# One store of a convolution cut into transfers of 112, 8 and 8 channels

## The chip, the cores and the metric

The kernel runs on one core of one Trainium2 chip. The metric is the device time of one execution in microseconds (us), and the time of a kernel is the median of several executions. TensorE (PE) multiplies, VectorE (DVE) adds, ScalarE (ACT) copies, GpSimd (POOL) casts and adds, and SyncE (SP) waits and issues transfers. The core has 16 DMA engines; SP, ACT and POOL each issue transfers into a queue of their own, and the same 16 engines serve all queues.

## The reference

A 3x3 convolution with padding 1, batch of 16 images, 64 input channels, 128 output channels, 64x64 pixels, in float32:

```python
x_pad = np.pad(x, ((0, 0), (0, 0), (1, 1), (1, 1)), mode='constant')
for b, co, ci, kh, kw:
    output[b, co] += weight[co, ci, kh, kw] * x_pad[b, ci, kh:kh+h, kw:kw+w]
```

(the five loops are written on one line here). The input is 16.8 MB, the output 33.6 MB.

## The kernel before

**The work and its tiling.** Images are worked on in eight pairs (`p` from 0 to 7). The two images of a pair lie in the two halves of the 128 partitions, 64 input channels each. Two output rows are made at a time from shared products: the middle row of the weights meets the sum of two neighbouring input rows (tile `ss`, made by POOL, or by DVE for the first pair), and the other products use differences of the weights' rows, made once at the start (`Wt`). A pair's 32 double rows are done in four blocks of eight.

**One block** (lines 129 to 190). Three groups of matmuls: `U` from the row sums, `A` for the upper rows, `Bt` for the lower rows. ACT copies `U` of both images from PSUM to SBUF (line 173). DVE adds it to `A` (line 183) and to `Bt` (line 186) and writes the output tile `ots[b2]`, 128 output channels by 64 rows by 64 columns in float32, 16 KB for each channel. There is one such tile for each image.

**Input.** SP issues the loads of the weights and of the first two pairs in float32 (lines 41 to 46). POOL issues the other six pairs, cast to 16 bits on the way (line 56), all of them in the first 8 us of the span.

**Output.** Each image is 2 MB. `cuts_of` (lines 112 to 114) says after which block which rows are stored: pairs 0 to 5 store each image whole after the last block; pair 6 stores its first image in two halves and its second whole; pair 7 stores both in halves. The first image of a pair is stored by SP right away (line 188). The second image's store is put on the list `held` (line 190) and issued by ACT in the next block, after ACT's pair of copies (lines 175 and 176), or after the last block (lines 191 and 192):

```python
while held:
    keep(store(nc.scalar, *held.pop(0)))
```

`keep` holds an instruction at its written place among those of its engine. So the second image of the sixth pair (`p` = 5) is issued by ACT in the first block of pair 6. Output tiles come from a pool of seven buffers; the tile of the sixth pair's second image is not used again by a later one. Each transfer raises a semaphore by 16 as its engines land; eight such semaphores go round among the transfers that SP and ACT issue, and at the end of the program (line 218) SP waits for all stores to have landed.

Of the kernel before, what the change touches and what calls it, by code (L numbers as in the profile page):

```python
# [13 lines left out]
def kernel(  # L14
# [8 lines left out]
    CO = weight.shape[0]  # L23
    assert H == 64 and W == 64 and CI == 64 and CO == 128 and B % 2 == 0
    NP = B // 2
# [4 lines left out]
    out_rows = out.rearrange("b co h w -> b co h w")  # L30
# [34 lines left out]
    def sums(eng, p, src, lo, n):  # L65
        if p not in ss:
            ss[p] = spool.tile([128, H // 2, W], F16, tag="ss", name="ss")
        v = src.rearrange("p (j i) c -> p j i c", i=2)
        keep(
            eng.tensor_add(  # L70
                ss[p][:, lo : lo + n, :], v[:, lo : lo + n, 0, :], v[:, lo : lo + n, 1, :]
            )
        )
# [21 lines left out]
    def cast(copy, p, src, lo, hi):  # L95
        keep(copy(xs[p][:, lo:hi, :], src[:, lo:hi, :]))  # L96
# [13 lines left out]
    held = []  # L110
# [2 lines left out]
    halves = {1: (0, 32), 3: (32, 64)}  # L113
    cuts_of = [(whole, whole)] * (NP - 2) + [(halves, whole), (halves, halves)]

    def store(eng, p, b2, ot, lo, hi):
        return eng.dma_start(
            out_rows[2 * p + b2, :, lo:hi, :],
            ot.rearrange("p j i c -> p (j i) c")[:, lo:hi, :],
        )  # L120

    for p in range(NP):
        if p + 1 < NP:
            for lo in (0, 16):
                sums(nc.gpsimd, p + 1, x1 if p == 0 else xs[p + 1], lo, 16)
        ots = [
            opool.tile([128, H // 2, 2, W], F32, tag="ot", name="ot") for _ in range(2)
        ]
        for blk in range(4):
            j0 = blk * RB  # L130

            def group(wi_rows):

                tiles = [
                    psum.tile([128, RB, W], F32, tag="acc", name="acc") for _ in range(2)
                ]
                n = 3 * len(wi_rows)
                i = 0
                for wi, off in wi_rows:
                    for kw in (1, 0, 2):  # L140
                        c_lo, c_hi = max(0, 1 - kw), min(W, W + 1 - kw)
                        for b2 in range(2):
                            p0 = 64 * b2
                            lo, hi = j0, j0 + RB
                            if off is None:
                                rhs = ss[p][p0 : p0 + 64, lo:hi, c_lo + kw - 1 : c_hi + kw - 1]
                            else:
                                while 2 * lo + off < 0:
                                    lo += 1
                                while 2 * (hi - 1) + off > H - 1:  # L150
                                    hi -= 1
                                first = 2 * lo + off
                                last = 2 * (hi - 1) + off
                                rhs = xs[p][
                                    p0 : p0 + 64,
                                    first : last + 1 : 2,
                                    c_lo + kw - 1 : c_hi + kw - 1,
                                ]
                            nc.tensor.matmul(  # L159
                                tiles[b2][:, lo - j0 : hi - j0, c_lo:c_hi],  # L160
                                Wt[p0 : p0 + 64, wi, kw, :],
                                rhs,
                                start=i == 0,
                                stop=i == n - 1,
                            )
                        i += 1
                return tiles

            U = group([(G1, None)])
            us = []  # L170
            for b2 in range(2):
                ut = upool.tile([128, RB, W], F32, tag="ut", name="ut")
                keep(nc.scalar.copy(ut, U[b2]))  # L173
                us.append(ut)
            while held:
                keep(store(nc.scalar, *held.pop(0)))
            for piece in later.get((p, blk), ()):
                cast(nc.scalar.copy, *piece)
            if p == 0 and blk < 3:
                sums(nc.vector, 0, x0, j0 + RB, RB)  # L180
            A = group([(G21, 1), (G0, -1)])
            for b2 in range(2):
                nc.vector.tensor_add(ots[b2][:, j0 : j0 + RB, 0, :], A[b2], us[b2])  # L183
            Bt = group([(G01, 0), (G2, 2)])
            for b2 in range(2):
                nc.vector.tensor_add(ots[b2][:, j0 : j0 + RB, 1, :], Bt[b2], us[b2])  # L186
            if blk in cuts_of[p][0]:
                store(nc.sync, p, 0, ots[0], *cuts_of[p][0][blk])
            if blk in cuts_of[p][1]:
                held.append((p, 1, ots[1], *cuts_of[p][1][blk]))  # L190
    while held:
        keep(store(nc.scalar, *held.pop(0)))

# [29 lines left out]
```

## Time and profile before

| | |
|---|---|
| median of 3 runs | 126.64 us (126.49 to 126.67) |
| the profiled execution | 126.7 us |
| its span, first to last instruction | 124.9 us |
| PE busy | 107.1 us (86%) |
| DVE busy | 83.4 us (67%) |
| ACT busy | 43.0 us (34%) |
| POOL busy | 36.9 us (30%) |
| queue q1 (issued by SP) | 2016 packets, 21.27 MB, 41.2% of 16 engines |
| queue q10 (issued by ACT) | 1296 packets, 16.78 MB, 31.7% |
| queue q0 (issued by POOL) | 864 packets, 6.29 MB, 24.3% |
| a whole image, ACT's queue: issue to landing | 18.2 us |
| a half image, ACT's queue: issue to landing | 8.3 us |

Engines' busy time leaves out what their sequencers do, such as issuing transfers. A queue's share is the time that its packets took, over the span of 16 engines. A packet of a store is one channel's contiguous row, 16 KB of a whole image or 8 KB of a half; the transfer ends with a packet of 4 bytes on each engine, which raises the semaphore. Two more queues, q8 and q14, bring instructions: seven packets of 16 KB and some of 8 KB over the span.

### The profile page before, as it was taken

The page shows a single profiled execution, that of the slowest core. Times are in us where ns is not written, and L with a number is a line of the kernel's source. Part 1 is how long each engine was busy: PE and PEld are TensorE (multiplying, and loading weights), DVE is VectorE, ACT ScalarE, POOL GpSimd, SP SyncE. Part 2 cuts the span into 40 slices and gives each one's busy share as a digit, 9 for nine tenths or more (in the row PEclk, how much of TensorE's full clock was granted, in tenths as well). Part 3 has the DMA queues.
Part 4 walks back from the last instruction along what each step waited for, and adds up shares of the span by engine and source line. Part 5 has one row for each costly group of instructions (what it writes and reads, how often), then busy time and mean ns, then how long its engine had stood idle before and what let it go on. Part 6 is the DMA issues. An engine that isn't in the chain of part 4 may idle for free.

```text
span 124.9 us, 2408 instructions
## 1 busy us (share of the span) xinstructions
PE 107.1 (86%) x978; PEld 53.9 (43%) x978; DVE 83.4 (67%) x134; ACT 43.0 (34%) x74; POOL 36.9 (30%) x29
## 2 busy tenths in 40 slices
PE   0489997399999999999999999999999999998000
PEld 0334443144545545555455555555555555553000
DVE  0135998227778777878877887877787778768200
ACT  4284234466333333333333333333333333333000
POOL 2845101999929101910048000750000000000000
PEclk9999999779999999999999999999999999999955
DMA  4999999999999999999999999999999999999991
GB/s 119 353 362 320 325 336 218 212 278 341 378 370 320 325 380 349 346 372 336 357 367 357 328 378 420 441 420 430 435 420 430 420 420 420 443 425 417 401 407 66
DMA packets 4187, 44.48 MB, mean 356 GB/s; under 512 B 465, under 2 KB 465, under 8 KB 721
## 3 DMA queue, kind: packets, MB, share of 16 engines
q1 hardware_dynamic: 2016, 21.27, 41.2%
q10 hardware_dynamic: 1296, 16.78, 31.7%
q0 software_dynamic: 864, 6.29, 24.3%
q8 instruction: 7, 0.11, 0.3%
q14 instruction: 4, 0.02, 0.0%
HBM read 17.07 MB, written 33.55 MB: 405 GB/s over the span
## 4 chain that ended last, share of the span: by engine, by line
PE 72%; DMA 15%; POOL 2%; DVE 1%; SPq 1%; issue 1%; DVEq 0%
PE acc L159 72%; DMA x<-in_x_dram 15%; POOL ss L70 2%; SPq L44 1%; DVE ot L183 1%; DVEq L218 0%; DVE ot L186 0%; SPq L41 0%; DVEq L183 0%
## 5 line engine op out<-in xcount | busy, mean ns | idle before, releaser
L159 PE MATMUL acc<-xs,Wt 64*128 64x504 f16 (+3 forms) x768 | 89.0, 379 | 0.0
L159 PEld LDWEIGHTS <-Wt 64*128 64x128 f16 x960 | 52.8, 96 | 56.2 <-issue 6.8
L183 DVE TENSOR_TENSOR ot<-acc,ut 128x512 f32<-128x512 f32 x64 | 41.2, 685 | 24.0 <-PE acc L159 21.7
L173 ACT COPY ut<-acc 128x512 f32<-128x512 f32 x64 | 34.4, 590 | 63.3 <-issue 41.7
L186 DVE TENSOR_TENSOR ot<-acc,ut 128x512 f32<-128x512 f32 x64 | 41.1, 683 | 0.0
L70 POOL TENSOR_TENSOR ss<-xs 128x1024 f16<-128x1024 f16 x12 | 25.2, 2125 | 31.7 <-DMA xs<-in_x_dram 31.7
L159 PE MATMUL acc<-ss,Wt 64*128 64x504 f16 (+1 forms) x192 | 27.6, 392 | 3.5 <-POOL ss L70 2.7
L70 DVE TENSOR_TENSOR ss<-x 128x512 f16<-128x512 f32 x4 | 2.7, 685 | 9.0 <-DMA x<-in_x_dram 9.0
L96 ACT CAST xs<-x 128x1024 f16<-128x1024 f32 (+1 forms) x6 | 6.3, 1067 | 3.1 <-DMA x<-in_x_dram 3.1
L70 POOL TENSOR_TENSOR ss<-x 128x1024 f16<-128x1024 f32 x2 | 4.7, 2344 | 8.4 <-DMA x<-in_x_dram 8.4
L88 PE MATMUL wp<-ident,w 128*64 128x128 f16 x18 | 1.3, 328 | 4.4 <-POOL w L50 4.4
L56 POOL DMA_DIRECT2D xs<-in_x_dram x6 | 3.3, 582 | 0.0
L96 POOL CAST xs<-x 128x1024 f16<-128x1024 f32 (+1 forms) x2 | 2.4, 1248 | 3.0 <-DMA x<-in_x_dram 3.0
L88 PEld LDWEIGHTS <-w 128*64 128x64 f16 x18 | 1.1, 210 | 4.4 <-POOL w L50 4.4
L90 ACT CAST Wt<-wp 128x384 f16<-128x384 f32 x1 | 0.5, 478 | 3.1 <-PE wp L88 3.1
L90 ACT ACT_TABLE_LOAD x1 | 1.3, 1283 | 0.7 <-PEq L207 0.7
L50 POOL CAST w<-w_raw 128x576 f16<-128x576 f32 x1 | 0.7, 663 | 2.4 <-DMA w_raw<-in_weight_dram 2.4
L99 ACT CAST Wt<-wp 128x384 f16<-128x384 f32 x1 | 0.5, 478 | 0.5 <-DVE Wt L93 0.5
L92 DVE TENSOR_TENSOR Wt<-wp,Wt 128x384 f16<-128x384 f32 x1 | 0.6, 550 | 0.0
L93 DVE TENSOR_TENSOR Wt<-wp,Wt 128x384 f16<-128x384 f32 x1 | 0.5, 547 | 0.0
L100 ACT CAST Wt<-wp 128x384 f16<-128x384 f32 x1 | 0.5, 485 | 0.0
masks.py:199 POOL TENSOR_SCALAR_AFFINE_SELECT ident<-ident 128x128 f16<-128x128 f16 x1 | 0.3, 292 | 0.1
(5 smaller groups left out, 0.6 us busy)
## 6 DMA issues: line engine op xcount, KB each, us to landing
out_dram<-ot ACTq DMA_DIRECT2D x7, 2048.0 KB, 18.2
out_dram<-ot SPq DMA_DIRECT2D x6, 2048.0 KB, 19.2
xs<-in_x_dram POOLq DMA_DIRECT2D x6, 1024.0 KB, 37.1
out_dram<-ot SPq DMA_DIRECT2D x4, 1024.0 KB, 9.2
x<-in_x_dram SPq DMA_DIRECT2D x1, 2048.0 KB, 19.3
out_dram<-ot ACTq DMA_DIRECT2D x2, 1024.0 KB, 8.3
x<-in_x_dram SPq DMA_DIRECT2D x1, 1472.0 KB, 9.0
x<-in_x_dram SPq DMA_DIRECT2D x1, 576.0 KB, 4.6
```

What stands on the lines that cost most here:

```text
L44: nc.sync.dma_start(x0[:, lo:hi, :], x_rows[0:128, lo:hi, :])
L50: keep(nc.gpsimd.tensor_copy(w16, w_raw))
L56: keep(nc.gpsimd.dma_start(xs[p], x_rows[128 * p : 128 * p + 128, :, :]))
L70: eng.tensor_add(ss[p][:, lo : lo + n, :], v[:, lo : lo + n, 0, :], v[:, lo : lo + n, 1, :])
L88: nc.tensor.matmul(wp[q : q + 64, k * CO : k * CO + CO], w16[:, t::9], ident)
L90: keep(nc.scalar.copy(wrow(G1), wps[1]))
L92: keep(nc.vector.tensor_sub(wrow(G21), wps[2], wrow(G1)))
L96: keep(copy(xs[p][:, lo:hi, :], src[:, lo:hi, :]))
L159: nc.tensor.matmul(tiles[b2][:, lo - j0 : hi - j0, c_lo:c_hi], Wt[p0 : p0 + 64, wi, kw, :], rhs, start=i == 0, stop=i == n - 1,)
L173: keep(nc.scalar.copy(ut, U[b2]))
L183: nc.vector.tensor_add(ots[b2][:, j0 : j0 + RB, 0, :], A[b2], us[b2])
L186: nc.vector.tensor_add(ots[b2][:, j0 : j0 + RB, 1, :], Bt[b2], us[b2])
```

## The change

`store` gets two more arguments, the first and the last channel, and stores only these. For `p == NP - 3`, the sixth pair, the entry of the second image on `held` becomes three: channels 0 to 112, 112 to 120 and 120 to 128. ACT issues the three transfers one after another where it issued one. All other stores have one entry with all 128 channels, as before. The bytes and their places in memory are the same. A transfer's channels are dealt out over the DMA engines, and the change is described as moving one row (16 KB) from each of engines 8 to 15 to engines 0 to 7.

```diff
-    def store(eng, p, b2, ot, lo, hi):
+    def store(eng, p, b2, ot, lo, hi, c0=0, c1=CO):
         return eng.dma_start(
-            out_rows[2 * p + b2, :, lo:hi, :],
-            ot.rearrange("p j i c -> p (j i) c")[:, lo:hi, :],
+            out_rows[2 * p + b2, c0:c1, lo:hi, :],
+            ot.rearrange("p j i c -> p (j i) c")[c0:c1, lo:hi, :],
         )
...
             if blk in cuts_of[p][1]:
-                held.append((p, 1, ots[1], *cuts_of[p][1][blk]))
+                edges = (0, 112, 120, CO) if p == NP - 3 else (0, CO)
+                for c in zip(edges, edges[1:]):
+                    held.append((p, 1, ots[1], *cuts_of[p][1][blk], *c))
     while held:
         keep(store(nc.scalar, *held.pop(0)))
```

## The prediction

> **What bounds the kernel now.** I read the page first, then the waits of the SP queue, then the last stretch of the span in windows, then ACT's timeline around the changed store, and last the single DMA packets of the trace.
>
> The page shows DMA full from the second slice to the last but one, beside a PE that is just as full. Its slices are 3.12 us long:
>
> ```profile
> PE   0489997399999999999999999999999999998000
> DMA  4999999999999999999999999999999999999991
> GB/s 119 353 362 320 325 336 218 212 278 341 378 370 320 325 380 349 346 372 336 357 367 357 328 378 420 441 420 430 435 420 430 420 420 420 443 425 417 401 407 66
> ```
>
> PE stops three slices ahead of DMA, so the end is not PE's. The page's chain of work ends with DVE and cannot say this, since it starts from the last compute instruction (DVE's, which ends at 116.42 us in a span of 124.92). The SP queue's waits from 115 us on show who has the end:
>
> ```profile
> SPq L218 <- DMA out_dram<-ot: 7.5, 4, 3.6
> ```
>
> SP stands 7.5 us in four waits for stores to land. The windows over the last stretch (columns: stretch, its length, busy time of PE, PEld, DVE, ACT and POOL, granted clock, DMA share, GB/s) show how the 16 engines run dry:
>
> ```profile
> 90.00:103.00 13.00, 13.00 (x126) 6.65 (x124) 10.23 (x18) 4.33 (x9) 0.00 (x0) 1.00 1.00 423
> 116.00:117.00 1.00, 0.00 (x0) 0.00 (x0) 0.42 (x1) 0.00 (x0) 0.00 (x0) 1.00 0.88 369
> 117.00:121.00 4.00, 0.00 (x0) 0.00 (x0) 0.00 (x0) 0.00 (x0) 0.00 (x0) 0.73 1.01 424
> 121.00:121.60 0.60, 0.00 (x0) 0.00 (x0) 0.00 (x0) 0.00 (x0) 0.00 (x0) 0.50 1.03 437
> 121.60:122.20 0.60, 0.00 (x0) 0.00 (x0) 0.00 (x0) 0.00 (x0) 0.00 (x0) 0.50 0.59 246
> 122.20:122.80 0.60, 0.00 (x0) 0.00 (x0) 0.00 (x0) 0.00 (x0) 0.00 (x0) 0.50 0.30 123
> 122.80:123.50 0.70, 0.00 (x0) 0.00 (x0) 0.00 (x0) 0.00 (x0) 0.00 (x0) 0.50 0.09 35
> ```
>
> The reader is to see two things. All engines are busy until 121.6, and then they stop at different times over 1.9 us. And there is a dip at 116 to 117 (0.88), in which some engines have nothing to do because SP's last store is not yet issued. An engine that is early there gets its time back for nothing; an engine that is late there never waits.
>
> The trace has each packet's queue, start, duration and size, not its engine. Packets of one engine follow each other closely (the next starts about 3 ns before the last ends: a 16 KB row every 0.611 us, an 8 KB half row every 0.306), so from the last packet back they can be strung into 16 lanes; I did that down to 85 us. By lane, the last packet starts or ends within 10 ns of these times:
>
> ```
> eight early lanes:  121.63 121.64 121.65 121.65 121.71 121.78 | 122.32 (fetch at 91.1)  122.78 (fetch at 103.7)
> eight late lanes:   121.68 122.45 122.57 122.60 122.77 122.82   123.28 123.50
> idle at 116.1 to 116.8, early lanes only: 0.15 0.23 0.30 0.36 0.48 0.69
> ```
>
> I sort them by when they finish the sixth pair's second image: 102.07 to 102.48 for seven early lanes, 102.98 to 103.99 for the late eight. The other early lane finishes it at 103.03, but carried a 0.88 us packet of the instruction queue (16 KB, at 91.1). Another of the early eight gets such a packet, 0.94 us, at 103.7. These two lost their early place through that and have no idle time at 116. The semaphore of the last store, whose steps are the engines' landings, says the same at the end: seven steps at 121.96 to 122.13, then 122.67 to 123.16, then 123.62 and 123.97. The last step is 0.47 us behind the last packet, SP goes on at 124.02, and the span ends 0.95 us after the landing.
>
> **The change part by part.** The profiled execution took 126.70 us (span 124.92 and 1.78 around it). The median of the three timed runs is 126.64, so I carry a difference over to that.
>
> *Two more issues on ACT's queue.* The three stores are issued at the place of the one, after the pair of copies at 90.16. ACT's timeline there:
>
> ```profile
> 90.16 1.07 ACT L173 COPY ut<-acc 128x512 f32<-128x512 f32 x2 [2.09 <-issue]
> 90.84 0.34 ACTq L117 DMA_DIRECT2D out_dram<-ot  x1
> 93.34 1.07 ACT L173 COPY ut<-acc 128x512 f32<-128x512 f32 x2 [2.10 <-DVE ot L186]
> ```
>
> An issue takes 0.34 and is preceded by a wait instruction of the queue, with some 0.1 between. Two more are 2 x 0.44 = 0.88: ACT is free again at 91.18 + 0.88 = 92.06 instead of 91.18, and the next copy starts at 93.34, held by DVE. Cost nothing; the cover is 2.1 us of ACT's idle time, without which it would be 0.88 on the copies that PE's buffers wait for. The queue's semaphores go round in eight: the two new stores take the places of stores that landed by 73.7, and every later store moves on by two places; the tightest of those, the last of all, issued at 116.45, would wait for a new small store, due about 104. Nothing waits. SP's stores and POOL's loads are not passed by anything.
>
> *Bytes.* None are added. 112 rows are 7 for each of 16 engines and the eights go to eight engines each, if the change does what it says: 9 rows on engines 0 to 7, 7 on 8 to 15. That is +0.611 us for eight lanes and -0.611 for the other eight. The small stores' own completion packets (9 ns each, two per low engine) are 0.02.
>
> [...]
>
> *The late lanes, if they are 8 to 15.* None of them idles at 116 except that the one at 121.68 would now begin to. Their ends move by -0.61: the last from 123.50 to 122.89, the next from 123.28 to 122.67.
>
> *The early lanes, if they are 0 to 7.* Six have 0.15 to 0.69 of idle time at 116, which hides part of the extra row: their ends become 121.78 to 122.10. The two with an instruction packet have none, and pay it all: 122.32 becomes 122.93, and 122.78 becomes 123.39, with the completion packets 123.40.
>
> *Sum.* The last packet ends at 123.40 instead of 123.50: -0.10 us. What is late next is the early lane that fetched instructions at 103.7; so five sixths of the 0.61 are lost to it. 126.64 - 0.10 = 126.54, which I call 126.5.
>
> *How long a row of 8 channels takes* is what the trace does not show. All its large transfers span 128 partitions. The two small stores put eight engines at once on eight neighbouring partitions. Lower bound: 0.611, as every row of before (a 16 KB packet of instructions costs more, 0.88 to 0.96). Upper bound: one after another, 8 x 0.611 = 4.89. I take 0.611, the row for the very same bytes by the same queue, and leave the upper end to the first rival. The same holds, more weakly, for how the 112 rows are dealt out.
>
> **The rivals.**
>
> *Engines in each other's way (slower).* Every engine of before carries 8 of the 128 rows of each store, and 16 x 16384 B / 0.611 us = 429 GB/s is what the full stretches show (423, 424). That fits a limit in the engines; it fits as well a memory that is read in 16 parts, one to an engine, and then eight neighbouring partitions lie in one to eight parts. Between 4.89 and 0.611 the middle in ratio is 1.73 us a row: 1.12 more, 2.24 for both rows, on lanes that all arrive within 0.4 us. On the fetching lane that gives 123.40 + 2.24 = 125.64, 2.14 later than now: 128.8. With two engines to a part (1.22 a row) it is 127.8, with four 130.2. It decides, that is, the kernel is slower by 0.2%, once the two rows together cost that lane 0.35 us more than 1.22. [...] Against it: no packet of a store is seen slower than its fellows by more than some tenths, whichever queues alternate.
> [...]
>
> *The late lanes are not 8 to 15 (slower).* Nothing in the trace numbers the engines. If the two latest lanes, or one of them, are among 0 to 7, a row is added to the last one: 123.28 + 0.63 or 123.50 + 0.63, that is 0.4 to 0.6 later: 127.0 to 127.3. For it: two lanes stand apart from the other fourteen, and one in each half would be as natural. Against it: the split is 8 to 8 once the two fetches are taken off, and a change of engine by halves explains eights.
> [...]
>
> *The instruction packet falls elsewhere (faster).* If the packet at 103.7 lands on a late lane or on an early one with idle time, the end is that of the other fetching lane, 122.93, or of the last late lane, 122.89: -0.57 to -0.61, 126.0 to 126.1. For it: the seven packets of this queue lie 12.4 to 16.7 us apart and the two I can place are on different lanes, so they wander. Against it: the program of PE, whose code is by far the longest, is unchanged, so they should wander the same way.
>
> **How the numbers follow.** Sum as above: 0.38, own range 126.3 to 126.7. Engines in each other's way: 0.33. Late lanes elsewhere: 0.14. Packet elsewhere: 0.15. About 0.2% (0.25 us) is what a measurement of this kernel can tell from no change; the three runs spread over 0.18. Faster by more: all of the last case and a quarter of the first (0.09), 0.24. Slower by more: 0.31 of the second case, all of the third and 0.03 of the first, 0.48. Within: 0.28. The range runs from 126.0, which leaves a third of the faster case below (0.05), to 129.2, which leaves the two-fifths of the second case above it where four engines or more share (0.13).
>
> **What would show it.** Right: two steps more of ACT's queue at 91 and the copy at 93.34 unmoved; in the windows, the dip at 116 to 117 nearly filled and the DMA share from 121.6 to 122.2 above 0.59, with nothing left after 123.4; every 16 KB packet at 0.61. The small stores' semaphores would take eight landings each, on the lanes that idled. Wrong: 16 KB packets of 1.2 us or longer near 101 to 104 us with the landings of the store at 90.8 spread beyond 104.4 (first rival); all packets at 0.61 but a last landing after 124.0 (second); an end below 123.0 with the 0.9 us packet on another lane (third).

## The result and the profile after

The changed kernel takes 132.19 us in the median against 126.66 for the one before: slower, ratio 1.044 with a 95% interval of 1.0377 to 1.0503, or 5.6 us (4.8 to 6.4). The forecast was 126.5 and the range ended at 129.2. Some executions of a kernel take some per cent longer than its others, and the ratio, like every one below, is taken without them on both sides.

The profiled execution has a span of 130.5 us. The page's busy lines after the change:

```profile
PE   0489998699999999999999999999999999900000
DMA  4999999999999999999999999999999979999930
GB/s 116 336 375 294 329 327 221 213 314 387 364 339 347 364 364 364 347 332 382 364 339 342 362 392 442 432 437 412 427 372 389 301 294 394 409 424 427 394 151 18
```

A slice is 3.26 us here. The DMA digits are still nines, and yet the GB/s fall from 412 to 442 in slices 25 to 29 to 372, 389, 301 and 294 in slices 30 to 33 (95 to 108 us), the stretch in which the sixth pair's stores run. Before, no slice there was under 420. So the engines are busy with the same bytes for longer. PE and DVE are no later than before: DVE's last addition ends at 115.2 us (116.4 before), and everything behind it is the stores. The SP queue's waits from 112 us on:

```profile
SPq L220 <- DMA out_dram<-ot: 14.2, 1, 14.2
```

SP stands 14.2 us in one wait for landings, where before four waits came to 7.5 (that view began at 115 us). The windows of the new kernel (stretch, length, busy time of PE, PEld, DVE, ACT, POOL, clock, DMA share, GB/s):

```profile
90.00:94.00 4.00, 4.00 (x40) 2.12 (x38) 3.08 (x5) 1.11 (x3) 0.00 (x0) 1.00 1.00 422
94.00:98.00 4.00, 4.00 (x41) 2.12 (x38) 3.27 (x7) 1.07 (x2) 0.00 (x0) 1.00 0.99 373
98.00:102.00 4.00, 4.00 (x42) 2.15 (x40) 3.27 (x6) 1.30 (x3) 0.00 (x0) 1.00 1.03 371
102.00:104.00 2.00, 2.00 (x22) 1.11 (x20) 1.42 (x3) 0.85 (x2) 0.00 (x0) 1.00 1.37 315
104.00:106.00 2.00, 2.00 (x22) 1.04 (x19) 1.53 (x3) 1.05 (x2) 0.00 (x0) 1.00 0.66 233
106.00:110.00 4.00, 4.00 (x40) 2.17 (x38) 2.65 (x5) 1.09 (x3) 0.00 (x0) 1.00 0.98 367
...
121.00:124.00 3.00, 0.00 (x0) 0.00 (x0) 0.00 (x0) 0.00 (x0) 0.00 (x0) 0.50 0.92 388
124.00:126.00 2.00, 0.00 (x0) 0.00 (x0) 0.00 (x0) 0.00 (x0) 0.00 (x0) 0.50 0.44 184
126.00:128.00 2.00, 0.00 (x0) 0.00 (x0) 0.00 (x0) 0.00 (x0) 0.00 (x0) 0.50 0.18 74
128.00:129.00 1.00, 0.00 (x0) 0.00 (x0) 0.00 (x0) 0.00 (x0) 0.00 (x0) 0.50 0.06 25
```

The same stretches of the kernel before:

```profile
94.00:98.00 4.00, 4.00 (x40) 2.03 (x38) 2.62 (x5) 1.48 (x3) 0.00 (x0) 1.00 0.98 418
98.00:102.00 4.00, 4.00 (x41) 2.08 (x38) 3.27 (x6) 1.07 (x2) 0.00 (x0) 1.00 1.00 428
102.00:104.00 2.00, 2.00 (x24) 1.04 (x21) 1.61 (x3) 1.03 (x2) 0.00 (x0) 1.00 1.00 418
104.00:106.00 2.00, 2.00 (x22) 1.04 (x20) 1.80 (x3) 0.04 (x1) 0.00 (x0) 1.00 0.99 410
```

Two stages are to be seen: 94 to 102 us at about 372 GB/s, while the store of 112 channels runs, and 102 to 106 us at 315 and 233 GB/s, while rows of the two small ones run. (A packet's whole time is counted where it begins, so the share of 1.37 and the 0.66 behind it are the same long packets.) At the end the engines run dry over 6 us, where before it took 1.9.

The single packets show it directly. Between 88 and 110 us, SP's and ACT's stores had 443 packets of 16 KB before, one over 0.7 us (beside a packet of instructions). After the change there are 410, 50 over 0.7 us, 22 over 1.2 us and the longest 4.35 us. Over all 16 engines from 88 us on, packets of stores took 49.9 us more than 0.611 and 0.309 each, against 3.0 before: 46.9 us more, or 2.9 for each engine, were they even. The last packet ends at 129.0 instead of 123.5, and this is the whole difference: the mean engine lost 2.9 us, the last one 5.5.

### The profile page after: what moved, and what is told of

Read it like the earlier page. It is cut to its first block, busy times and chain, and to the rows that moved or that the text cites. A ratio compares the mean times of both kernels' runs of the same rounds, so it can differ in the third digit from the quotient of the medians.

```text
span 130.5 us, 2410 instructions
## 1 busy us (share of the span) xinstructions
PE 106.4 (82%) x978; PEld 55.7 (43%) x978; DVE 83.4 (64%) x134; ACT 43.0 (33%) x74; POOL 36.9 (28%) x29
## 4 chain that ended last, share of the span: by engine, by line
PE 68%; DMA 15%; POOL 2%; DVE 1%; SPq 1%; issue 1%; DVEq 0%
PE acc L159 68%; DMA x<-in_x_dram 15%; POOL ss L70 2%; SPq L44 1%; DVE ot L183 1%; DVE ot L186 0%; DVEq L220 0%; SPq L41 0%; DVEq L183 0%
## 5 line engine op out<-in xcount | busy, mean ns | idle before, releaser
L159 PEld LDWEIGHTS <-Wt 64*128 64x128 f16 x960 | 54.6, 95 | 53.4 <-issue 5.6
L159 PE MATMUL acc<-ss,Wt 64*128 64x504 f16 (+1 forms) x192 | 27.1, 384 | 3.1 <-POOL ss L70 1.8
```

What stands on the lines that cost most here:

```text
L159: nc.tensor.matmul(tiles[b2][:, lo - j0 : hi - j0, c_lo:c_hi], Wt[p0 : p0 + 64, wi, kw, :], rhs, start=i == 0, stop=i == n - 1,)
```

## The experiments

The explanation to be tested is the prediction's first rival: engines wait for each other when they read neighbouring partitions at the same time. Other explanations are that small transfers are slow whatever they read; that a row is dear to an engine that is not its usual one; that the cut of 112 alone is to blame; and that the late lanes were not 8 to 15 (second rival). A lane is one DMA engine's string of packets, as in the prediction. Times are given by the ratio to the kernel before on the same chip.

### Two small stores on top, from four sets of partitions

In these four kernels the store of 128 channels is left whole. Two transfers of 8 rows follow it in ACT's queue and write to a place of the last image which that image's own store overwrites later. By the count of rows all put two (2 x 0.61 us) on eight engines, as the small stores of the change did, which had eight landings each; only the partitions differ. (The helper `again`, a store of chosen partitions, is left out below; each kernel has one of the four `EXTRA` lines.)

```diff
             while held:
                 keep(store(nc.scalar, *held.pop(0)))
+            while more:
+                keep(again(nc.scalar, *more.pop(0)))
...
+                if p == NP - 3:
+                    more.extend((ots[1], rows, d0) for rows, d0 in EXTRA)
...
+    EXTRA = [((112, 120, 1), 0), ((120, 128, 1), 8)]   # neighbouring
+    EXTRA = [((96, 112, 2), 0), ((97, 113, 2), 8)]     # every second
+    EXTRA = [((64, 96, 4), 0), ((96, 128, 4), 8)]      # every fourth, upper half
+    EXTRA = [((0, 32, 4), 0), ((32, 64, 4), 8)]        # every fourth, lower half
```

Neighbouring partitions:

> The store of the sixth pair's second image is whole as before; two transfers of 8 channels come on top of it, read from partitions 112 to 119 and 120 to 127 and written to a place of the last image that its own later store overwrites. So engines 0 to 7 carry two rows (2 x 0.61 us) more than before. Crowding (engines that read neighbouring partitions at once wait for each other; blocks of four partitions, so four engines to a part): about 2.4 us a row, the lane that fetched instructions ends at 122.8 + 4.9 = 127.7, 4.2 us later: 130.8. Cut of 112 alone to blame: the eights cost their bytes, 122.8 + 1.2 = 124.0 against 123.5, +0.5: 127.2. Small transfers slow whatever they read: as slow as crowding has it, but then the same in all three kernels of this kind.

Every second:

> As the kernel with the eights from neighbouring partitions, but the two transfers read partitions 96, 98, ... 110 and 97, 99, ... 111, so that in blocks of four two engines share a part. Crowding: 1.22 us a row, 122.8 + 2.4 = 125.2, +1.7: 128.4. Cut of 112 alone to blame: 127.2. Small transfers slow: the same as with neighbouring partitions.

Every fourth, lower half:

> As before it, but the two transfers read partitions 0, 4, ... 28 and 32, 36, ... 60: one to a block of four. Crowding: 0.61 us a row, no long packet, 122.8 + 1.2 = 124.0, +0.5: 127.2. Small transfers slow: the same as with neighbouring partitions. It also tells which lanes are engines 0 to 7, by the two more completion packets: if they are the late ones, the end moves by 1.2 to 127.9, if the early ones by 0.5.

Every fourth, upper half:

> [...] Crowding by blocks: engines 0 to 7 do not meet each other, only the home engine of each block, so between one and two engines to a part: 0.61 to 1.22 us a row; 127.9 (the kernel with partitions 0 to 60) to 128.4 (two engines to a part). If what costs is that a row is foreign to its engine, whatever the crowd: like the kernel with partitions 112 to 127, 131.5.

Measured (long packets: 16 KB, over 0.7 us, between 88 and 110 us; the surplus is summed over all engines' store packets from 88 us on; one of the long ones in each kernel, perhaps two in the first, stands behind a packet of instructions, as before):

```
                     ratio to before (95%)      us     long packets, longest   surplus, us
neighbouring         1.0324 (1.0258 to 1.0390)  +4.1   13, 2.52                16.4
every second         1.0097 (1.0060 to 1.0133)  +1.2    6, 1.27                 4.7
every fourth, upper  1.0105 (1.0076 to 1.0134)  +1.3    1, 1.01                 3.1
every fourth, lower  1.0067 (1.0039 to 1.0095)  +0.9    1, 0.99                 2.9
kernel before                                           1, 1.02                 3.0
```

The windows of the kernel with neighbouring partitions, and then of the one with every fourth, lower half:

```profile
102.00:104.00 2.00, 2.00 (x22) 1.08 (x20) 2.00 (x4) 0.07 (x1) 0.00 (x0) 1.00 0.97 336
104.00:106.00 2.00, 2.00 (x22) 1.03 (x19) 1.27 (x3) 1.01 (x2) 0.00 (x0) 1.00 1.18 397
106.00:108.00 2.00, 2.00 (x22) 1.02 (x18) 1.76 (x3) 0.84 (x2) 0.00 (x0) 1.00 0.80 332
```

```profile
102.00:104.00 2.00, 2.00 (x23) 1.13 (x20) 1.93 (x4) 0.72 (x2) 0.00 (x0) 1.00 0.91 385
104.00:106.00 2.00, 2.00 (x23) 1.03 (x19) 1.49 (x3) 0.36 (x1) 0.00 (x0) 1.00 1.03 426
106.00:108.00 2.00, 2.00 (x22) 1.08 (x20) 1.27 (x3) 1.07 (x2) 0.00 (x0) 1.00 1.04 438
```

The same bytes in the same count of transfers cost 4.1 us or 0.9, by the partitions alone. So it is not that the transfers are small. Nor is it that a row is foreign to its engine: neither half of the partitions, read at every fourth, has a long packet but the usual one. The longest row from neighbouring partitions took 2.52 us, about four times 0.61, and from every second 1.27, about twice. The expectations had 2.4 and 1.22, by four engines and by two to a part of four partitions. That a part has four was the author's assumption; the longest packets agree with it, and no run shows the parts themselves. In time, two to a part cannot be told from one (1.0097 against 1.0105 and 1.0067); with every second partition only five of the 16 rows were long. The expected times stood on a kernel before of 126.6, while its median in this set is 126.98, so the increases are what to compare. Every second partition gave +1.2, where +1.7 was expected. The lower half gave +0.9, between the 0.5 expected for early lanes and the 1.2 for late ones, so this kernel alone does not tell which lanes are engines 0 to 7.

### The 112 channels alone

```diff
-                edges = (0, 112, 120, CO) if p == NP - 3 else (0, CO)
+                edges = (0, 112) if p == NP - 3 else (0, CO)
```

> The sixth pair's second image is stored for channels 0 to 112 alone; the last 16 channels of it are left out. Every engine carries one row less than before (7 for 8). If the dealing of 112 rows over the engines is harmless: the late lanes end 0.61 earlier, -0.6: 126.0, and no packet of that store over 0.7 us but one beside a fetch. If the 112 rows are themselves crowded (rows dealt so that engines meet on the same part): rows of 0.9 to 2 us while the store runs, 1 to 2 us later in sum: 127.5 to 129.

This kernel leaves out the last 16 channels of that image. Measured: ratio 1.0055 (1.0011 to 1.0099), +0.7 us (0.1 to 1.3), with one row less on each engine by the count (7 for 8), so how the rows are dealt costs, by estimate, about 0.7 + 0.6 = 1.3 us. (The executions spread from 126.81 to 130.26, and the profiled one took 129.57, so its packets are to be read for their kind and not for their sum.) Its packets: 53 of 16 KB over 0.7 us, 16 over 1.2, the longest 2.11; a surplus of 30.2 us. The windows:

```profile
94.00:98.00 4.00, 4.00 (x41) 2.07 (x37) 3.27 (x7) 1.07 (x2) 0.00 (x0) 1.00 1.10 397
98.00:102.00 4.00, 4.00 (x42) 2.20 (x40) 3.09 (x6) 1.90 (x4) 0.00 (x0) 1.00 0.97 338
102.00:104.00 2.00, 2.00 (x22) 1.10 (x20) 1.60 (x3) 0.24 (x1) 0.00 (x0) 1.00 0.90 315
```

So the first stage of the loss is this one. The changed kernel shows it too: from 94 to 101 us, before the first row of a small store has landed (103.3), 25 of its 16 KB packets took over 0.7 us, up to 2.24. Of these, 12 belong to SP's whole store, so the other queue's rows are slow as well. That engines meet on the same partitions' part here is the likely reading, by the kernels above; how the 112 rows are dealt the trace does not tell.

### Cuts that move nothing

```diff
-                edges = (0, 112, 120, CO) if p == NP - 3 else (0, CO)
+                edges = (0, 112, CO) if p == NP - 3 else (0, CO)    # 112 and 16
+                edges = (0, 64, CO) if p == NP - 3 else (0, CO)     # 64 and 64
```

> The sixth pair's second image in two transfers, 112 and 16 channels, instead of three: every engine has 8 rows as before, none is moved. The 112 alone cost 1.2 us more than before with a row less, so about 1.9 us. Crowding: the 16 rows lie on 4 blocks' parts, four engines each, 2.4 us a row instead of 0.61 on every engine, so 1.9 + 1.8 = 3.7: 130.7. If only the moved rows and the two eights of the change were dear: 128.9.

> The sixth pair's second image in two transfers of 64 channels. Every engine has 8 rows as before. Crowding: 64 neighbouring partitions are half of the parts, two engines to a part, 1.22 us a row instead of 0.61; 8 rows are 4.9 us longer at most, half of that hidden behind the other queue's rows when they take turns: +2.4 to +4.9, 129.4 to 131.9. If every engine can read any partition at full rate as long as the count of rows is even: no change, 127.0.

Measured: 64 and 64, ratio 1.0357 (1.0317 to 1.0397), +4.5 us. For 112 and 16 there is no interval: its executions took 129.73, 131.68, 131.85 and 132.62 against a median of 126.75, so its fastest execution is 3.0 us behind. That is clear of no loss, but it lies between the 128.9 and the 130.7 that were to be told apart and does not decide between them. By the count of rows both kernels leave every engine its 8 (7 and 1, 4 and 4), and both are slow; 64 and 64 loses four fifths of what the change lost. The windows of 64 and 64:

```profile
94.00:98.00 4.00, 4.00 (x42) 2.11 (x38) 3.27 (x6) 1.32 (x3) 0.00 (x0) 1.00 1.02 344
98.00:102.00 4.00, 4.00 (x42) 2.23 (x40) 2.84 (x5) 1.91 (x4) 0.00 (x0) 1.00 1.03 324
102.00:104.00 2.00, 2.00 (x22) 1.04 (x19) 1.85 (x4) 0.00 (x0) 0.00 (x0) 1.00 0.95 225
104.00:106.00 2.00, 2.00 (x21) 1.03 (x18) 1.27 (x3) 1.07 (x2) 0.00 (x0) 1.00 0.96 238
```

From 102 to 106, where two thirds of the bytes are those of ACT's queue, the engines move 225 to 238 GB/s, a little over half of the 418 and 410 before: with half of the partitions, some half of the rate. That the count of rows is even on all engines does not help.

### Which engine is which

Three tiny transfers of 15, 8 and 7 channels with 64, 128 and 192 bytes a channel stand behind ACT's last store and mark the lanes.

```diff
+    rows = sixth.rearrange("p j i c -> p (j i) c")
+    for c, k, n in ((0, 15, 16), (16, 8, 32), (32, 7, 48)):
+        keep(nc.scalar.dma_start(out_rows[2 * NP - 5, c : c + k, 0, 0:n], rows[c : c + k, 0, 0:n]))
```

> The kernel before with three tiny transfers behind ACT's last store, of 15, 8 and 7 channels and 64, 128 and 192 bytes a channel, which write once more what already stands there. [...] My sum had the eight early lanes as 0 to 7 and the two latest among 8 to 15. [...]

In this first one the places written overlapped (channels from 0 on in all three), so the second transfer was issued only at 124.75, after the first had landed, and the kernel took 130.12 us. Only the 64 byte packets were of use: one follows the latest lane. The diff above is that of the second one, in which the places are apart.

> The kernel before with three tiny transfers behind ACT's last store as in the first kernel of this kind, which wrote over each other's place, so that the second and third waited for the first; here their places are apart, and all three are on the lanes before these run dry. [...] My sum: the lanes with a 128 byte packet end at 121.6 to 122.8, the others are the late ones with the two latest. [...]

Measured (127.68 us, one execution). The marks are nested: 15 lanes have a packet of 64 bytes, 8 of these 128, and 7 of these 192. No trace numbers the engines, so the lanes go by their marks here, and the 8 with 128 bytes, on which a transfer of 8 channels runs, are taken for the prediction's 0 to 7. The completion packets of the last store:

```
64, 128 and 192 bytes:  121.08 121.38 121.61 122.32 122.35 122.55 123.36
64 and 128:             121.29
64 alone:               121.22 121.52 122.65 122.75 122.78 122.85 123.13
no mark:                122.37
```

The latest lane (123.36) is among the 8 with 128 bytes and the second latest (123.13) among the others. The two groups differ in the mean (121.99 against 122.41), but the end is set by one lane, and that one gets a row more, if the small stores run on these 8, as the marks in the changed kernel (below) have it. So the change would have made the kernel slower even with rows of 0.611, by an estimate of 0.4 us: two uncrowded rows on eight engines cost 0.9, and this is half of it. The estimate rests on one marked execution, and no run gave those engines a single row more.

The changed kernel with the same marks:

> The changed kernel with the same three tiny transfers at its end. Crowding of the eights: the lanes with a 128 byte packet (engines 0 to 7) end last, 2 to 4 us behind the median of the others; the others are late by the dealing of the 112 alone, some 1 us. If both halves were held up alike, by the 112 rows alone, the two groups end side by side, the low one 1.2 us later.

Measured (133.43 us, one execution): the lanes with 64 bytes alone complete their last store at 123.13 to 125.99, the middle one at 124.74. Of the lanes with 128 bytes, the first completes at 125.73, the second at 128.03, and the marks of the other six stand at 128.7 to 129.5. These 8 are behind by about 4 us, the upper end of what was expected, and more than the 1.2 of two rows at 0.611: it is the eights that hold it up.

### The same cut earlier

```diff
-                edges = (0, 112, 120, CO) if p == NP - 3 else (0, CO)
+                edges = (0, 112, 120, CO) if p == 1 else (0, CO)
```

> The same cut into 112, 8 and 8 channels, at the second pair's second image (issued at about 52 us) instead of the sixth's. If time lost there is made good before the end, since the engines that fall behind can catch up while the others wait for PE: less than 1 us, under 128. If the engines are short of time all through, as the page's DMA line of nines has it: the whole 5.5 us, 132.

Measured: ratio 1.0501 (1.0439 to 1.0562), +6.4 us. The expectation had the place wrong (ACT issues this store at 38.4 us, not at 52; its rows run from about 43 us on, and packets over 0.7 us are frequent from 46 to 67), which changes nothing in the question. Time lost there is not made good before the end. The page's lines:

```profile
DMA  4999999999999999999999999999999999999920
GB/s 138 330 353 307 318 338 208 220 295 363 365 355 328 365 358 315 280 293 270 340 345 340 355 370 415 455 405 445 425 410 460 403 423 433 418 428 418 380 95 18
```

Now slices 16 to 19 (49 to 62 us) are the low ones, with 315, 280, 293 and 270 where the kernel before had 336 to 372, and from 95 us on no packet is long but the usual one. The end is as late all the same, as the line of nines in the DMA row had it: DMA is short of time from the first loads to the last store.

## Why the prediction was wrong

**What held.** The end is that of the stores, and DMA is short of time throughout: what the latest engine loses in its packets, the kernel loses. ACT's two more issues are hidden, though by less than I wrote. ACT's timeline after the change:

```profile
88.97 1.07 ACT L173 COPY ut<-acc 128x512 f32<-128x512 f32 x2 [2.09 <-issue]
89.65 2.38 ACTq L117 DMA_DIRECT2D out_dram<-ot  x3
92.14 1.07 ACT L173 COPY ut<-acc 128x512 f32<-128x512 f32 x2 [2.10 <-DVE ot L186]
```

The three issues took 0.34, 1.05 and 0.90 us and ended at 92.02, 0.12 before the next copy. I had 0.44 for each of the two. The count of the rows held as well: the semaphore of each small store stepped once as its issue ended and then eight times, at 103.3 to 108.0 and 104.8 to 110.9; that of the 112 channels has 16 landings, at 102.1 to 106.0.

**The step that failed first** is "how long a row of 8 channels takes", where I took 0.611, the row for the same bytes on the same queue. In the kernel before, that row was seen only in stores that span all 128 partitions. Read from neighbouring partitions the rows took up to 2.52 us with the rest whole, and up to 4.35 in the change. In its place: crowding costs 0.0324 - 0.0067 = 0.0257 of 127.0 us, 3.3 us (neighbouring partitions against every fourth; 3.6 by the medians, 131.49 against 127.90).

**The second** is the half sentence that the same holds "more weakly" for the 112 rows. I gave it no price and it is no term of any rival; it cost about 1.3 us (an estimate, from the kernel with 112 channels alone).

**The third** is "the late lanes, if they are 8 to 15". I had sorted the lanes 8 to 8 by their place at the sixth pair's store and took the two eights for the halves of the engines. No run shows the numbers of the engines. The marks show that the 8 lanes on which a transfer of 8 channels runs end interleaved with the other 8, and that the latest of all in that execution (123.36) is one of these 8. The second rival had one of the two latest there and priced it at 0.4 to 0.6; one uncrowded row costs, by the estimate above, about 0.4 (half of 0.9).

The three together are 3.3 + 1.3 + 0.4 = 5.0 us, against 5.6 (4.8 to 6.4) measured. That they simply add up is assumed.

**The rivals and the range.** The first rival was right that neighbouring partitions cost time (4.1 us against 0.9 to 1.3 from every second or fourth) and got 0.33, less than my forecast (0.38), although the one point held against it, that no row of the kernel before was slow, says nothing about transfers of fewer partitions. The sign named for it came: packets of 16 KB of 1.2 us and longer, and landings up to 110.9 instead of 104.4. Its price of 1.73 us a row, the middle in ratio, was too low: the longest row from neighbouring partitions with the rest whole, 2.52, agrees with the 2.44 of four engines to a part, which I had put at 130.2. The range stopped at 129.2 on the strength of that middle. And a range to 130.2 would not have held the time either: each case was priced with the others at nothing, while here three costs came together. The third rival, the packet of instructions, played no part that these runs show: it fell at 89.9 and 103.3, much as before.

**Open:** how 112 rows are dealt over 16 engines; why single rows of the change took up to 4.35 us, where the small stores alone had 2.52; and what makes single lanes late in the kernel before, by up to 1.9 us. None of these was tried.

## What to carry to other kernels

What a transfer cost here was set by which partitions it read (4.1 us for two stores of 8 neighbouring rows, 0.9 to 1.3 for every second or fourth), and not by bytes and engine counts alone: in the kernel before, stores of all 128 channels kept 0.611 us a row, and every cut by channels that was tried lost time, even into two even halves (3.6%). A profile in which every large transfer spans all partitions cannot price one that does not; such a cost is better taken at its upper end, and two unpriced costs are to be added before the range is drawn. And where a few late lanes set the end, it must be known which they are (a few marked bytes behind the last store sorted them here, 8 from 8) before work is moved between them.

## What was not expected of the hardware

An issue on ACT's queue with none right before it took 0.33 to 0.39 us (once 0.53, the first 64 channels), but one right behind another took 0.29 to 1.6: 1.05 and 0.90 for the eights of the change, 1.11 for the 16 channels behind 112, 1.32 for the second 64, 1.60 for the first small store of every fourth partition, lower half. So it is not the count of 8 rows that makes it dear. What makes it so was not tried.

A crowded transfer slows the other queue as well. In the changed kernel, from 88 us on, SP's packets of 16 KB, all from whole stores, took 7.4 us more than 0.611 each in sum, against 0.4 in the kernel before, and ACT's 37.4, against 1.2.
